# Sums of the seven-product weight factors: each written over another part, and issued one split ahead of its cast

## The chip, the cores and the metric

The kernel runs on one core of a Trainium2 chip. The metric is the device time of one execution in microseconds (us); of the kernel before there are three runs, with a median of 2215.59 us.

The engines are TensorE (PE: matrix products; PEld its weight loads), VectorE (DVE), ScalarE (ACT), GpSimd (POOL) and SyncE (SP, which issues most DMAs). Each engine works through its own queue in the order of the program. An instruction whose semaphores are not up yet holds up all that stands behind it in the same queue.

## What is computed

One inference step of a two-layer trunk: an mLSTM mixer with a SwiGLU feed-forward part, then sliding-window attention with a second SwiGLU part, for 1024 prompt rows and 32 sample rows of width 1024. Nothing but the two feed-forward parts is touched by the change:

```python
def swiglu(x, w_gu, w_down):
    g, u = jnp.split(x @ w_gu, 2, axis=-1)
    return (jax.nn.silu(g) * u) @ w_down
...
x = layer_norm(DEEPNORM_ALPHA * x + swiglu(x, w_gu[layer], w_down[layer]), ln_g[layer, 1], ln_b[layer, 1])
```

`w_gu` is 1024 x 5632 in each layer, `w_down` 2816 x 1024, all in float32.

## The kernel before

**Three products for one.** Each float32 operand is split in a high part, rounded to the matrix unit's type by a cast, and a low part, the difference. `gemm` (lines 360 to 371) issues high x high, high x low and low x high for every 128-row tile. A weight split is one cast on ACT (line 208) and one difference on POOL, for some weights on DVE (line 210).

**Seven products for eight.** Most of the feed-forward weights come in pairs of loaded units, `a` and `b`, each of 128 x 1024. Their halves a1, a2, b1, b2 (128 x 512) are the blocks of a 2 x 2 block matrix. Strassen's scheme in Winograd's form takes seven products of such blocks in place of eight. Its weight factors are four of the blocks' own and sums of them: a1, a2, b2, s1 = b1 + b2, s2 = s1 - a1, s3 = a1 - b1, s4 = a2 - s2. They are split in the order of `FACTORS` (line 135): a1, a2, b2, s2, s1, s3, s4. They are used in the order a1, a2, s2, b2, s1, s3, s4.

**Where the sums are made.** All four are 128 x 512 subtractions or additions on DVE, in place in the loaded tiles. `_source` issues them just ahead of the split that it is called for: `a1 -= b1` at b2's split (line 176, this is s3), `b1 += b2` and `b2 -= a1` at s2's split (lines 179 and 180, s1 and s2), `a2 -= b2` at s1's split (line 182, s4). The second of s2's sums overwrites b2, so it has to wait until b2's cast and difference, issued one split before, have read it.

**When a split is issued.** There are five buffers for split parts (`SLOTS`). In the stretches with pairs no split is paced by time: `done` (line 234), called when the products of a factor have been issued, takes the factor off the list and issues the next splits until four are held. So a split runs four factors ahead of PE: with the products of s3 of a pair behind it, `done` issues b2 of the next pair, with those of s4 its s2, with a1's the next s1, with a2's s3, and with s2's s4.

**The up stage** (`up_tile`, lines 342 to 401, 20 pairs in each layer) computes gate and up columns. A factor is 24 matmuls of 264 columns over 4 tiles and two column halves. The banks are of two kinds, A and B, two buffers each. In A a sum of products grows over a1, s2, s1 and s4, and ACT copies it out between them (lines 1362, 1372, 1379), which PE's next product in A has to wait for. B takes a2, b2 and s3, and DVE adds it to the copies (lines 1367, 1375, 1382, 1383; line 1384 multiplies gate and up, line 1390 is the second gate's activation and line 1397 its product). `done` for a factor stands ahead of these instructions. Beside this `stage` splits the results as the next product's moving operand and writes them to memory (cast at line 1288, difference at 1289, DMA at 1290; sums at 1300 to 1313).

**The down stage** (`down`, lines 1480 to 1521, 8 pairs in each layer). A factor is two halves (q) of 12 matmuls. Each half has a bank: A keeps one buffer per half over a1, s2, s1, s4, and B takes a2, b2, s3. After each half DVE puts the bank into the residual (`put`, lines 1487 to 1493), once or, for s3, twice. The next half into the same buffer waits for the put that reads it. A pair's first half writes the buffer that s4's first half of the pair before wrote. Here `done` follows the puts of the factor:

```python
                for q in range(2):
                    ...
                    for row, par in outs:
                        put(ps, 4 * j + 2 * q + row, par)
                ...
                W.done(u, f)
```

**Names in the trace.** `wr` are loaded units, `wh` and `wl` split parts (`_a`, `_b`, `_s` from the factor's first letter), `z` and `ex`, `sx` buffers of activations, `act` the residual, `hs_x` and `hs_t` the staged operands in memory.

Of the kernel before, what the change touches and what calls it, by code (L numbers as in the profile page):

```python
# [69 lines left out]
class Weave:  # L70


    def __init__(self):
        self.tasks = []
        self.feed = None
# [53 lines left out]
class Weights:  # L129
# [7 lines left out]
    def __init__(self, nc, pool, units, pairs, on_vector):  # L137
        self.nc, self.pool, self.units, self.on_vector = nc, pool, units, on_vector
        self.nload = self.njob = 0
        self.raw, self.parts, self.home, self.live = {}, {}, {}, set()  # L140
        self.jobs, self.last = [], {}
        self.wait, self.ahead, self.pause = 0.0, False, FEED_W
        self.depth = RAW - 1
        self.spare, self.spared = None, set()
        u = 0
        while u < len(units):
            if u in pairs:
                self.jobs += [(u, f) for f in self.FACTORS]
                self.last[u] = self.last[u + 1] = len(self.jobs) - 1
                u += 2  # L150
            else:
                self.jobs += [(u, 0), (u, 1)]
                self.last[u] = len(self.jobs) - 1
                u += 1
# [11 lines left out]
    def _source(self, u, f):  # L166

        n = self.units[u].shape[-1] // 2
        if f in (0, 1):
            return self.raw[u][:, f * n : (f + 1) * n]  # L170
        sub, add = self.nc.vector.tensor_sub, self.nc.vector.tensor_add
        a, b = self.raw[u], self.raw[u + 1]
        a1, a2, b1, b2 = a[:, :n], a[:, n : 2 * n], b[:, :n], b[:, n : 2 * n]
        if f == "b2":

            sub(a1, a1, b1)
        elif f == "s2":

            add(b1, b1, b2)
            sub(b2, b2, a1)  # L180
        elif f == "s1":
            sub(a2, a2, b2)
        return {"a1": a1, "a2": a2, "b2": b2, "s1": b1, "s2": b2, "s3": a1, "s4": a2}[f]

    def _next(self):
        if self.njob == len(self.jobs):
            return False
        key = self.jobs[self.njob]
        u, f = key
        if key not in self.home and len(self.live) == SLOTS and (self.spared or not self.spare):  # L190
            return False
        if key in self.home and any(self.home.get(k) is self.home[key] for k in self.parts):
            return False
        self.load_to(u if f in (0, 1) else u + 1)
        r = self._source(u, f)
        w = r.shape[-1]
        if key in self.home:
            hi, lo = self.home[key]
        else:
            if self.spare and not self.spared:  # L200
                self.spared.add(key)
                at, tag, bufs = self.spare, "x", 1
            else:
                self.live.add(key)
                at, tag, bufs = self.pool, "", SLOTS
            hi = at.tile([P, WD // 2], F32R, name=f"wh{u}_{f}", tag="wh" + tag, bufs=bufs)[:, :w]
            lo = at.tile([P, WD // 2], F32R, name=f"wl{u}_{f}", tag="wl" + tag, bufs=bufs)[:, :w]
        self.nc.scalar.copy(hi, r)  # L208
        eng = self.nc.vector if key in self.on_vector else self.nc.gpsimd
        eng.tensor_sub(lo, r, hi.bitcast(F32))  # L210
        self.parts[key] = (hi, lo)
        self.njob += 1
        if f in (1, "s4"):
            del self.raw[u]
            if f == "s4":
                del self.raw[u + 1]
                u += 1
            self.load_to(u + self.depth)
        return True

    def split_to(self, i):
# [1776 lines left out]
```

## Time and profile before

| | us |
|---|---|
| median of 3 runs (lowest, highest) | 2215.59 (2215.38, 2216.78) |
| the profiled execution, its own time | 2219.82 |
| its span, first to last instruction | 2218.0 |
| PE busy in the span | 2178.0 |
| DVE busy | 1468.7 |
| POOL busy | 1020.5 |
| ACT busy | 1002.6 |

The granted TensorE clock of the profiled execution is 0.997. A row of instructions names its line, engine and operation, then output<-input by the program's names, the shapes and a count, then the time in which the group was busy, the mean length of one in ns, and the idle time of the engine just before them with the instruction that ended most of it. In a timeline a row begins with start and length in us from the start of the span; instructions of the same kind in a row are merged, with their count. Matmuls overlap in their records, so the distance from start to start tells PE's pace, and not their length.

### The profile page before, as it was taken

Reading aid. Unit: us, or ns where it says so; the run is one execution under the profiler, and the core shown is the slowest. Engines: PE = TensorE matmul, PEld = TensorE weight load, DVE = VectorE, ACT = ScalarE, POOL = GpSimd, SP = SyncE. Lnnn points to the kernel's source line nnn. Section 1 sums busy time; section 2 is a strip of 40 time slices with the busy share of each in tenths; the row PEclk is TensorE's granted clock in tenths of the full one; section 3 lists DMA queues with packets and bytes.
Section 4 is the critical chain, followed back from the end, with each engine's and each line's share of the span. In section 5 each row is a group of like instructions: output and inputs, shape, how many; then the busy total and the mean of one; then the engine's idle time right before and its main releaser. Section 6 shows DMA issues by size and latency. Waiting matters only on the chain.

```text
span 2218.0 us, 44293 instructions
## 1 busy us (share of the span) xinstructions
PE 2178.0 (98%) x17086; PEld 2149.8 (97%) x17086; DVE 1468.7 (66%) x2848; ACT 1002.6 (45%) x2259; POOL 1020.5 (46%) x982
## 2 busy tenths in 40 slices
PE   9999999999999999999998999999999999999997
PEld 9999999999999999999998999899999999999997
DVE  4465677787666665566667678888576666466657
ACT  4443455464344444321245778756444444422125
POOL 2544210004666566544525776600576666554441
PEclk9999999999999999999999999999999999999999
DMA  5221212212443343797515333521244434397712
GB/s 169 78 62 57 57 39 86 89 39 80 153 155 136 137 155 136 248 333 230 175 57 173 108 100 97 155 63 39 103 162 163 135 138 155 129 343 258 243 59 79
DMA packets 174500, 298.10 MB, mean 134 GB/s; under 512 B 18065, under 2 KB 130761, under 8 KB 174289
## 3 DMA queue, kind: packets, MB, share of 16 engines
q1 hardware_dynamic: 169936, 290.94, 39.9%
q10 hardware_dynamic: 4352, 4.33, 0.6%
q8 instruction: 135, 2.21, 0.4%
q14 instruction: 77, 0.62, 0.1%
HBM read 201.80 MB, written 82.94 MB: 128 GB/s over the span
## 4 chain that ended last, share of the span: by engine, by line
PE 61%; DVE 5%; ACT 3%; DMA 2%; issue 2%; POOL 2%; SPq 0%; POOLq 0%; DVEq 0%; ACTq 0%
PE A L368 9%; PE A L370 9%; PE A L369 9%; PE B L368 6%; PE B L369 6%; PE B L370 6%; PE d L368 4%; PE d L370 4%; PE d L369 4%; PE T L1763 1%; POOL s L1743 1%; DMA hs_x<-z 1%; DMA sx<-hs_t 1%; ACT act L471 1%; PE O L1778 1%
## 5 line engine op out<-in xcount | busy, mean ns | idle before, releaser
L210 POOL TENSOR_TENSOR wl_s<-wr,wh_s 128x512 fp32r<-128x512 f32 x224 | 316.6, 1433 | 262.6 <-ACT wh_s L208 187.6
L210 POOL TENSOR_TENSOR wl_a<-wr,wh_a 128x512 fp32r<-128x512 f32 x112 | 168.7, 1513 | 386.7 <-ACT wh_a L208 264.5
L368 PE MATMUL d<-sx,wh 128*128 128x264 f32 (+2 forms) x1068 | 341.3, 320 | 2.1 <-ACT wh L208 1.6
L370 PE MATMUL d<-sx,wl 128*128 128x264 f32 (+2 forms) x1068 | 325.7, 305 | 2.8 <-POOL wl L210 2.8
L369 PE MATMUL d<-sx,wh 128*128 128x264 f32 (+2 forms) x1068 | 324.8, 304 | 0.4 <-DVE sx L399 0.4
L208 ACT CAST wh_s<-wr 128x512 fp32r<-128x512 f32 x224 | 136.0, 619 | 323.4 <-DVE wr L180 295.6
L368 PE MATMUL A<-sx,wh_s 128*128 128x264 f32 x896 | 254.8, 284 | 1.8 <-ACT z L1372 1.8
L369 PE MATMUL A<-sx,wh_s 128*128 128x264 f32 x896 | 254.2, 284 | 0.0
L370 PE MATMUL A<-sx,wl_s 128*128 128x264 f32 x896 | 254.0, 284 | 0.0
L368 PEld LDWEIGHTS d<-sx,wh 128*128 128x128 f32 x1068 | 201.9, 189 | 5.8 <-ACT wh L208 2.3
L370 PEld LDWEIGHTS d<-sx,wl 128*128 128x128 f32 x1068 | 201.3, 189 | 4.2 <-POOL wl L210 3.9
L369 PEld LDWEIGHTS d<-sx,wh 128*128 128x128 f32 x1068 | 202.1, 189 | 1.5 <-DVE sx L399 0.7
L368 PE MATMUL d<-sx,ex 128*128 128x264 f32 x624 | 180.5, 289 | 0.1
L369 PE MATMUL d<-sx,ex 128*128 128x264 f32 x624 | 177.2, 284 | 0.0
L370 PE MATMUL d<-sx,ex 128*128 128x264 f32 x624 | 176.9, 284 | 0.0
L368 PEld LDWEIGHTS A<-sx,wh_s 128*128 128x128 f32 x896 | 168.4, 188 | 2.4 <-ACT z L1372 2.2
L370 PEld LDWEIGHTS A<-sx,wl_s 128*128 128x128 f32 x896 | 168.8, 188 | 0.0
L369 PEld LDWEIGHTS A<-sx,wh_s 128*128 128x128 f32 x896 | 168.4, 188 | 0.0
L1289 POOL TENSOR_TENSOR z<-z 128x528 fp32r<-128x528 f32 x76 | 104.8, 1378 | 113.4 <-ACT z L1288 106.8
L210 POOL TENSOR_TENSOR wl<-wr,wh 128x512 fp32r<-128x512 f32 (+2 forms) x81 | 104.1, 1293 | 93.1 <-ACT wh L208 89.3
L1743 POOL TENSOR_SCALAR s<-s,st 128x256 f32<-128x256 f32 (+1 forms) x144 | 123.1, 867 | 47.9 <-DVE st L1741 32.0
L1288 ACT CAST z<-z 128x528 fp32r<-128x528 f32 x136 | 86.1, 633 | 94.2 <-DVE z L1301 39.1
(348 smaller groups left out, 7307.3 us busy)
## 6 DMA issues: line engine op xcount, KB each, us to landing
wr<-in_gu SPq DMA_DIRECT2D x92, 512.0 KB
hs_x<-z SPq DMA_DIRECT2D x72, 528.0 KB
hs_t<-z SPq DMA_DIRECT2D x64, 528.0 KB
sx<-hs_x SPq DMA_DIRECT2D x112, 264.0 KB
sx<-hs_t SPq DMA_DIRECT2D x64, 264.0 KB
ex<-hs_t SPq DMA_DIRECT2D x64, 264.0 KB
wr<-in_dn SPq DMA_DIRECT2D x32, 512.0 KB
ex<-hs_x SPq DMA_DIRECT2D x32, 264.0 KB
```

Of the source, the lines that this page charges most:

```text
L208: self.nc.scalar.copy(hi, r)
L210: eng.tensor_sub(lo, r, hi.bitcast(F32))
L368: nc.tensor.matmul(out, ah, bh, start=start and k == 0, stop=False, **kw)
L369: nc.tensor.matmul(out, ah, bl, start=False, stop=False, **kw)
L370: nc.tensor.matmul(out, al, bh, start=False, stop=stop and k == last, **kw)
L471: nc.scalar.activation(z, z, AF.Identity, scale=gk, bias=bk)
L1288: nc.scalar.copy(hi.bitcast(F32R), buf(s))
L1289: eng.tensor_sub(lo.bitcast(F32R), buf(s), hi)
L1743: nc.gpsimd.tensor_scalar_mul(p[:R, h, lo:256], p[:R, h, lo:256], st[:R, 2, h : h + 1])
L1763: nc.tensor.transpose(pt[:nk, i, h, :R], p[:R, h, c : c + nk], ident[:R, :R])
L1778: nc.tensor.matmul(po[:, :, :R], v, s["hi"][:nk, i, :, :R], start=(i == 0), stop=False)
```

## The change

The same four sums are made from other parts. s1 still goes over b1. s2 is now b1 - a1 and goes over a1, s3 is b2 - s2 and goes over b2, and s4 is a2 - s2 over a2. No sum overwrites a part whose split has been issued immediately before it. They are issued by a new function, `prepare`, which `_next` calls at its end for the split that comes next, and which `_source` calls where this has not happened. So the two sums for s2 stand behind the split of b2, the one for s3 behind the split of s1, and the one for s4 behind the split of s3. The order of the splits is as before.

```diff
+        self.made = set()
...
         if f in (0, 1):
             return self.raw[u][:, f * n : (f + 1) * n]
+        self.prepare(u, f)
+        a, b = self.raw[u], self.raw[u + 1]
+        return {
+            "a1": a[:, :n], "a2": a[:, n : 2 * n], "b2": b[:, n : 2 * n],
+            "s1": b[:, :n], "s2": a[:, :n], "s3": b[:, n : 2 * n], "s4": a[:, n : 2 * n],
+        }[f]
+
+    def prepare(self, u, f):
+
+        if (u, f) in self.made or f not in ("s2", "s3", "s4"):
+            return
+        self.made.add((u, f))
         sub, add = self.nc.vector.tensor_sub, self.nc.vector.tensor_add
+        n = self.units[u].shape[-1] // 2
         a, b = self.raw[u], self.raw[u + 1]
         a1, a2, b1, b2 = a[:, :n], a[:, n : 2 * n], b[:, :n], b[:, n : 2 * n]
-        if f == "b2":
-
-            sub(a1, a1, b1)
-        elif f == "s2":
-
+        if f == "s2":
             add(b1, b1, b2)
+            sub(a1, b1, a1)
+        elif f == "s3":
             sub(b2, b2, a1)
-        elif f == "s1":
-            sub(a2, a2, b2)
-        return {"a1": a1, "a2": a2, "b2": b2, "s1": b1, "s2": b2, "s3": a1, "s4": a2}[f]
+        else:
+            sub(a2, a2, a1)
...
             self.load_to(u + self.depth)
+        if self.njob < len(self.jobs):
+            u, f = self.jobs[self.njob]
+            if u in self.raw and u + 1 in self.raw:
+                self.prepare(u, f)
         return True
```

## The prediction

> **What bounds the kernel now.** I read the page first, then TensorE's (PE's) waits, the 14 places at which one down pair follows another, and the up stages' few gaps.
>
> ```profile
> span 2218.0 us, 44293 instructions
> PE 2178.0 (98%) x17086; PEld 2149.8 (97%) x17086; DVE 1468.7 (66%) x2848; ACT 1002.6 (45%) x2259; POOL 1020.5 (46%) x982
> L208 ACT CAST wh_s<-wr 128x512 fp32r<-128x512 f32 x224 | 136.0, 619 | 323.4 <-DVE wr L180 295.6
> ```
>
> PE is busy for 98% of the span, so 295.6 us of ScalarE (ACT) idling behind the sum of line 180 is mostly not a cost: what counts is where PE itself stops. The stretch and its busy times, then the waits of PE in the down stage of the first layer and the sums there (count; shortest, median, longest ns):
>
> ```profile
> 955.00:1090.00 135.00, 135.00 (x1114) 135.00 (x1113) 89.59 (x130) 28.38 (x48) 63.74 (x48) 1.00 0.75 243
> PE A L368 <- DVE act L1491: 1.1, 1, 1.1
> L176 DVE TENSOR_TENSOR wr<-wr,wr x6: 684/684/686, 971.9 to 1073.9; 128x512 f32<-128x512 f32 x6
> L176 DVE TENSOR_TENSOR wr<-wr,wr x6: 685/686/686, 2004.6 to 2106.5; 128x512 f32<-128x512 f32 x6
> ```
>
> PE has no visible hole in 135 us; VectorE (DVE) is busy for 89.59. But a busy average hides who arrives with nothing to spare. One boundary between two down pairs, on DVE, GpSimd (POOL) and PE (start, duration):
>
> ```profile
> 989.65 2.77 DVE L1493 TENSOR_TENSOR act<-act,B 128x528 f32<-128x528 f32 x4 [0.75 <-PE B L370]
> 992.34 0.68 DVE L176 TENSOR_TENSOR wr<-wr,wr 128x512 f32<-128x512 f32 x1
> 992.94 0.70 DVE L1493 TENSOR_TENSOR act<-act,A 128x528 f32<-128x528 f32 x1
> 994.00 0.71 DVE L1493 TENSOR_TENSOR act<-act,A 128x528 f32<-128x528 f32 x1 [0.36 <-PE A L370]
> 994.62 0.68 DVE L179 TENSOR_TENSOR wr<-wr 128x512 f32<-128x512 f32 x1
> 995.41 0.69 DVE L180 TENSOR_TENSOR wr<-wr,wr 128x512 f32<-128x512 f32 x1
> 996.02 0.70 DVE L1493 TENSOR_TENSOR act<-act,A 128x528 f32<-128x528 f32 x1
> ...
> 988.82 1.29 POOL L210 TENSOR_TENSOR wl_b<-wr,wh_b 128x512 fp32r<-128x512 f32 x1 [1.67 <-ACT wh_b L208]
> ...
> 993.68 0.28 PE L370 MATMUL A<-sx,wl_s 128*128 128x264 f32 x1
> 993.80 0.34 PE L368 MATMUL A<-ex,wh_a 128*128 128x264 f32 x1
> 993.98 0.28 PE L369 MATMUL A<-ex,wh_a 128*128 128x264 f32 x1
> ```
>
> The matmul at 993.80 opens the next pair and overwrites bank A's first buffer, which the put at 992.94 has to read out first (s4's first half). That put ends at 993.64, 0.16 before the matmul. At the first boundary, where PE does wait:
>
> ```profile
> 951.56 0.69 DVE L176 TENSOR_TENSOR wr<-wr,wr 128x512 f32<-128x512 f32 x1
> 952.16 1.31 DVE L1491 SCALAR_TENSOR_TENSOR act<-act,A 128x528 f32<-128x528 f32 x2
> ...
> 951.67 0.28 PE L370 MATMUL A<-sx,wl_s 128*128 128x264 f32 x1
> 953.01 0.36 PE L368 MATMUL A<-sx,wh_a 128*128 128x264 f32 x1 [1.06 <-DVE act L1491]
> 953.21 0.28 PE L369 MATMUL A<-sx,wh_a 128*128 128x264 f32 x1
> ```
>
> The first of the two puts lasts 952.16 + 0.70 (the other put's length) = 952.86, and PE goes 0.15 later. So a lag of 0.15 is the signal itself, and 0.16 at the steady boundary means that DVE meets PE's pace with 0.01 us left. I read PE as bounded by DVE's queue there, though no view calls it a wait.
>
> **The change part by part.** Four sums per pair before, four after; casts, differences on POOL and loads stay, and their order too. What moves is where the sums stand in DVE's queue.
>
> *Behind s3.* The split of the next pair's b2 is issued when s3's products are done. Before, one sum went with it (line 176, at 992.34). Now two do, `b1 += b2` and `a1 = b1 - a1`, the second needing the first. From L176 to the put is 0.60 start to start. From L179 to L180, where the second also waits for the first, is 995.41 - 994.62 = 0.79, and from L180 to the put 0.61. So the put of s4 moves from +0.60 to 0.79 + 0.61 = +1.40: 0.80 later. Queued behind it are s4's second put and a1's puts; who waits is PE's first matmul of the next pair. There are 8 down pairs in a layer, 7 boundaries, so 14 (the six L176 per window above and one at 951.56, twice). 14 x 0.80 = 11.2, less the slack: 0.01 at 993.80, none at the two waiting boundaries; I allow 0.02 at each of the other 12, 0.3 in all. **Loss 10.9.** Lower end: sums that start 0.60 apart, 14 x 0.60 - 0.3 = 8.1. Upper end: after a real wait PE's second matmul also comes late, 953.21 - 953.01 = 0.20 against a pitch of 0.12 (993.80 less 993.68), adding 0.08 at 12 boundaries: 11.9.
>
> The Trainium skill, VectorE: DVE Perf Modes, section The DRAIN you can't avoid, says that a semaphore between consecutive VectorE operations adds nothing to their distance. By it the second sum would start 0.60 after the first and the loss would be the 8.1. The rows disagree, 0.79 where one waits for the other, so I keep 0.80.
>
> *Behind s4.* L179 and L180 vanish there, 1.4 us of DVE. In the down stage the next puts wait for PE anyway (0.36 idle before 994.00), so it is worth nothing. If POOL's queue or ACT's were what PE awaited it would be worth up to 1.4 a pair; the down stage shows no such wait.
>
> *s3's and s4's sums.* `b2 -= a1` stands where line 182 stood (behind a1's products), `a2 -= a1` one factor on, behind a2's. In the down stage 0.7 to 1.8 us (the longest sum, below) goes ahead of s2's puts. Those have until s1 reuses their buffer, three half factors of 12 x 0.12 = 1.46, or 4.4 us, and take 0.70 each: covered; uncovered, it would cost up to 1.8 - 0.7 a pair. In the up stage it goes ahead of the addition at line 1367, whose bank is not wanted for several factors.
>
> *The cast freed.* s2's cast waits no longer on sums issued beside it. Here PE's gaps in the up stages matter: first tile, then third, of layer one.
>
> ```profile
> 526.93 0.28 PE L370 MATMUL B<-sx,wl_a 128*128 128x264 f32 x1
> 527.10 0.39 PE L368 MATMUL A<-ex,wh_s 128*128 128x264 f32 x1
> 527.32 0.28 PE L369 MATMUL A<-ex,wh_s 128*128 128x264 f32 x1
> 527.84 0.40 PE L370 MATMUL A<-ex,wl_s 128*128 128x264 f32 x1 [0.24 <-POOL wl_s L210]
> ...
> 574.22 0.28 PE L370 MATMUL B<-ex,wl_b 128*128 128x264 f32 x1
> 575.84 0.39 PE L368 MATMUL A<-sx,wh_s 128*128 128x264 f32 x1 [1.34 <-ACT z L1372]
> ```
>
> The first three intervals are 0.91 instead of 0.36: 0.55 lost, with 0.1 more on the restart. The other is 1.62 instead of 0.12: 1.50. Layer two, PE's waits in its up stage:
>
> ```profile
> PE A L368 <- ACT z L1372: 0.4, 1, 0.4
> PE A L368 <- ACT z L1362: 0.2, 1, 0.2
> PE A L370 <- POOL wl_s L210: 0.2, 1, 0.2
> ```
>
> The wait view counts from a matmul's modelled end, 0.16 less than start to start (1.34 against 1.50), so these are about 0.6, 0.4 and 0.4. All four gaps hold 0.65 + 1.5 + 1.4 = 3.6. Why the third tile stalls:
>
> ```profile
> 564.58 0.69 DVE L180 TENSOR_TENSOR wr<-wr,wr 128x512 f32<-128x512 f32 x1
> ...
> 565.36 0.62 ACT L208 CAST wh_s<-wr 128x512 fp32r<-128x512 f32 x1 [6.64 <-DVE wr L180]
> 565.88 0.60 ACT L1390 ACTIVATE z<-A 128x528 f32<-128x528 f32 x1
> ...
> 567.84 1.79 DVE L1289 TENSOR_TENSOR z<-z 128x528 fp32r<-128x528 f32 x1
> ...
> 574.14 0.63 ACT L1288 CAST z<-z 128x528 fp32r<-128x528 f32 x1 [0.76 <-DMA hs_t<-z]
> ...
> 575.20 0.59 ACT L1372 COPY z<-A 128x528 f32<-128x528 f32 x1
> ```
>
> ACT sits 6.64 on the cast with the activation of line 1390 right behind, then a staging write, its DMA, and the copy for which PE waits. With both sums ahead of lines 1382 to 1384 the activation comes earlier, and the copy has 1.5 us to win. **Gain**: the first tiles in full (0.65 and 0.8), two thirds of the third tiles' 2.1, since line 1289 and the DMA may start less early: 2.9. Ends: 0, and 3.6. Late next would be the same copy; the three rows are all of PE's waits in that stage, so nothing else there is near its path.
>
> *Contended sums.* In the up stage a sum beside POOL takes longer:
>
> ```profile
> 638.84 1.77 DVE L176 TENSOR_TENSOR wr<-wr,wr 128x512 f32<-128x512 f32 x1
> 643.14 0.70 DVE L1382 TENSOR_TENSOR z<-z,B 128x528 f32<-128x528 f32 x1 [2.53 <-PE B L370]
> ```
>
> Two of these are 3.5 us, until 642.4, inside the 2.53 us for which DVE waits for s3's products before line 1382: nothing. Without that cover they would delay line 1382 by up to 1.8 a tile, whose bank PE wants only several factors later.
>
> **The sum.** 10.9 - 2.9 = +8.0 on the profiled execution's 2219.82 (span 2218.0 and 1.8 around it): 2227.8. That execution lies 4.2 above the median of the three runs, 2215.59, so the forecast for the median is **2223.6**. Ends: 8.1 - 3.6 = +4.5, 2220.1; and +11.9, 2227.5.
>
> **The rivals.** *Misplaced sums (the other side).* The two sums could come out a factor away from s3's puts, if the count of held parts put b2's split elsewhere. Then the put follows s3's puts at once, no boundary pays, the two waiting ones even win 0.60: -1.2 - 2.9 = -4.1, 2211.5. It decides from the point where DVE's queue has no sum between line 1493's four puts and s4's. For it: nothing but that the function is called anew. Against: L176 stands there in all rows, and the number of splits held is untouched.
>
> *Nothing extra for the dependence.* 8.1 - 2.9 = +5.2, 2220.8. Against it the 0.79. That is the rule of the Trainium skill named above.
>
> *Contention at the boundary.* If a POOL difference ran under the two sums, each could take 1.77 and not 0.68: one or both of them 1.09 longer at 14 places, 15 to 31 us on top of the 8, 2239 to 2254. Against: b2's difference ends at 990.11, 2.2 us before the sums. The Trainium skill, SBUF — State Buffer, section Who interferes with whom, has a VectorE operation with two SBUF inputs fully blocked by a GpSimd one that reads SBUF. The 1.77 agrees; only a moved POOL operation would bring it here.
>
> *The gain falls out.* The freed cast could let staging reach its DMA no earlier: +10.9, 2226.5.
>
> **How the numbers follow.** The forecast's case 0.72 (own range 2221 to 2226.5), the gain falling out 0.08, no price for dependence 0.06, misplaced 0.09, contended 0.05. What a measurement here can tell from no change is 0.2%, 4.4 us: 2211.2 to 2220.0. Slower: 0.72 + 0.08 + 0.05, and two thirds of 0.06, less 0.04 for the forecast case's tail, 0.85. Misplaced divides evenly at its -4.1: 0.05 faster, and the remaining 0.10 is same. For 8 in 10 the range runs from 2219.0 to 2228.0: it leaves out misplaced, contended and thin tails.
>
> **What would show it.** Between line 1493's four puts and s4's first put, two sums with a put 1.4 after the first; a wait of PE of about 0.8 at each of 14 boundaries, named after DVE's lines 1491 and 1493; no wait of ACT on the line of the sums like the 295.6; PE's waits at s2 in the first tiles gone, and at line 1372 smaller. Wrong: boundaries without a gap, a different sum there, or durations of 1.8.

## The result and the profile after

The changed kernel takes 2224.3 us (median of 6 runs, 2223.07 to 2229.09), the kernel before, on the same chip, 2217.16 (6 runs, 2215.38 to 2219.97). The ratio is 1.0035, with a 95% interval from 1.0022 to 1.0048: slower by 7.1 us. The prediction was 2223.6, with a range of 2219.0 to 2228.0.

The page of the changed kernel (its profiled execution took 2223.39 us): span, busy times, and the group of the weight casts, now line 219.

```profile
span 2221.5 us, 44254 instructions
PE 2177.9 (98%) x17086; PEld 2150.1 (97%) x17086; DVE 1448.6 (65%) x2848; ACT 1008.5 (45%) x2259; POOL 985.0 (44%) x982
L219 ACT CAST wh_s<-wr 128x512 fp32r<-128x512 f32 x224 | 136.8, 618 | 226.4 <-DVE wr L192 64.0
```

Most of the page looks better. DVE and POOL are busy for less, and the row of ACT's casts names 64.0 us of idling behind a sum where it named 295.6. (A row names its largest wait only. With 29.7 and 13.8 us behind the other sums ACT idles 107.5 us.) PE, the one that counts, has not changed its busy time and has a longer span.

Stage by stage it becomes plain. The timeline of PE, first in the kernel before, then in the changed one: the first matmul of the up stage, the first of the down stage and the last of the down stage, in layer one.

```profile
521.21 0.28 PE L368 MATMUL A<-sx,wh_a 128*128 128x264 f32 x1
...
931.49 0.28 PE L368 MATMUL A<-sx,wh_a 128*128 128x264 f32 x1
...
1095.73 0.28 PE L370 MATMUL A<-sx,wl_s 128*128 128x264 f32 x1
```

```profile
520.62 0.28 PE L383 MATMUL A<-sx,wh_a 128*128 128x264 f32 x1
...
928.66 0.28 PE L383 MATMUL A<-sx,wh_a 128*128 128x264 f32 x1
...
1098.62 0.28 PE L385 MATMUL A<-sx,wl_s 128*128 128x264 f32 x1
```

The up stage (`up_tile`, lines 1342 to 1401 of the kernel before) takes 928.66 - 520.62 = 408.04 instead of 410.28, the down stage 169.96 instead of 164.24. The same distances for both layers of every kernel of this study follow, in us, each from one profiled execution (five kernels repeat 408.04 and 408.30 to 0.01); "sum" is the difference of the four stages to the kernel before, "median" the difference of the medians, each to the kernel before on the same chip:

| kernel | up 1 | down 1 | up 2 | down 2 | sum | median |
|---|---|---|---|---|---|---|
| before | 410.28 | 164.24 | 410.00 | 164.65 | | |
| changed | 408.04 | 169.96 | 408.30 | 169.62 | +6.8 | +7.1 |
| e1_in_place | 412.58 | 164.27 | 412.43 | 163.53 | +3.6 | +2.3 |
| e2_two_sooner | 408.04 | 165.33 | 408.31 | 165.34 | -2.2 | -1.5 |
| e3_old_sums_ahead | 408.04 | 173.35 | 408.31 | 171.26 | +11.8 | +14.2 |
| e4_one_more | 410.86 | 170.96 | 410.96 | 169.31 | +12.9 | +11.9 |
| e5_up_ahead | 408.04 | 163.44 | 408.31 | 164.07 | -5.3 | -5.8 |
| e6_one_more_late | 409.75 | 164.13 | 409.65 | 164.20 | -1.4 | +0.3 |
| e7_one_each | 408.04 | 167.39 | 408.30 | 167.33 | +1.9 | +1.0 |

The change loses 5.72 + 4.97 = 10.69 in the down stages and gains 2.24 + 1.70 = 3.94 in the up stages. (The two spans differ by 3.5 only, because the first stage began 0.59 earlier and the stretch between the layers, which the change doesn't touch, took 455.29 instead of 457.95. That stretch lies between 455.1 and 459.4 in the nine profiles.)

The boundary that the prediction showed, in the changed kernel, on DVE, ACT, POOL and PE:

```profile
988.65 2.77 DVE L1508 TENSOR_TENSOR act<-act,B 128x528 f32<-128x528 f32 x4 [0.75 <-PE B L385]
991.34 0.69 DVE L189 TENSOR_TENSOR wr<-wr 128x512 f32<-128x512 f32 x1
992.11 0.69 DVE L190 TENSOR_TENSOR wr<-wr,wr 128x512 f32<-128x512 f32 x1
992.72 1.31 DVE L1508 TENSOR_TENSOR act<-act,A 128x528 f32<-128x528 f32 x2
...
992.90 1.14 ACT L219 CAST wh_s<-wr 128x512 fp32r<-128x512 f32 x2 [5.16 <-PE A L384]
...
987.81 1.29 POOL L221 TENSOR_TENSOR wl_b<-wr,wh_b 128x512 fp32r<-128x512 f32 x1 [1.66 <-ACT wh_b L219]
...
992.68 0.28 PE L385 MATMUL A<-sx,wl_s 128*128 128x264 f32 x1
993.57 0.36 PE L383 MATMUL A<-ex,wh_a 128*128 128x264 f32 x1 [0.61 <-ACT wh_s L219]
993.76 0.29 PE L384 MATMUL A<-ex,wh_a 128*128 128x264 f32 x1
```

Two sums stand between s3's four puts and s4's first. The second starts 0.77 after the first, and the put at 992.72, 1.38 after the first sum. With the 0.70 of one put it ends at 993.42, and PE goes 0.15 later, at 993.57. PE's distance is 0.89 where it was 0.12, and the next matmul comes 0.19 later and not 0.12. All twelve boundaries without a wait before now have 0.82 to 0.89; the two that had one went from 1.34 to 2.27 and from 1.46 to 1.97.

PE's waits, over the whole span (total us, times, longest), name another engine:

```profile
PE A L383 <- ACT wh_s L219: 10.5, 14, 2.0
```

Fourteen waits, as many as boundaries, and 10.5 us, but put down to ACT's cast of s2. The matmul at 993.57 reads `wh_a`, not `wh_s`, which speaks against it; but the first of the two casts at 992.90, 0.62 long, ends at 993.52 and the put at 993.42, so time alone doesn't tell the two apart here. The other places say more. In all six waits of PE for ACT that the profile of the kernel before shows, PE starts 0.05 after the end of the cast or copy. Here it starts 0.05 after the end of the cast at eight of the fourteen places, but 0.01 after it at the other six (the second, fourth and sixth boundary of each layer), which is too soon. Behind the end of the put the lag is 0.15 at the eight and 0.10 at the six. That speaks for the put; whether the put or the cast holds PE is the first question to the experiments.

### The profile page after: what moved, and what is told of

Same layout as the page of the kernel before. It is cut to its first block, busy times and chain, and to the rows that moved or that the text cites. A ratio compares the mean times of both kernels' runs of the same rounds, so it can differ in the third digit from the quotient of the medians.

```text
span 2221.5 us, 44254 instructions
## 1 busy us (share of the span) xinstructions
PE 2177.9 (98%) x17086; PEld 2150.1 (97%) x17086; DVE 1448.6 (65%) x2848; ACT 1008.5 (45%) x2259; POOL 985.0 (44%) x982
## 5 line engine op out<-in xcount | busy, mean ns | idle before, releaser
L221 POOL TENSOR_TENSOR wl_s<-wr,wh_s 128x512 fp32r<-128x512 f32 x224 | 298.7, 1337 | 267.3 <-ACT wh_s L219 256.9
L221 POOL TENSOR_TENSOR wl_a<-wr,wh_a 128x512 fp32r<-128x512 f32 x112 | 153.5, 1373 | 398.0 <-ACT wh_a L219 274.2
L383 PE MATMUL A<-ex,wh_s 128*128 128x264 f32 x448 | 127.4, 284 | 0.0
```

What stands on the lines that cost most here:

```text
L383: nc.tensor.matmul(out, ah, bh, start=start and k == 0, stop=False, **kw)
```

## The experiments

The theory: the price is DVE's queue at one place, the put of s4 behind s3's puts; whatever stands ahead of it there costs its length. Rivals: PE waits for s2's cast on ACT, as the wait view has it; or the kernel is slower for DVE's load or the new aliasing (s2 now goes over a1 and s3 over b2; s1 and s4 stay over b1 and a2), wherever the sums stand. The gain of the up stages is a second question: does it come from issuing ahead, or from the other parts? Diffs are against the changed kernel, except for e4 and e6, which are against the kernel before.

**e1_in_place: the new parts, each sum issued by its own split.**

```diff
-        if self.njob < len(self.jobs):
-            u, f = self.jobs[self.njob]
-            if u in self.raw and u + 1 in self.raw:
-                self.prepare(u, f)
```

> The new sums, but each issued at its own split, none ahead: s2's two sums then stand behind s4's puts, and no sum at all between s3's four puts and s4's first put. Theory (PE loses its time at the boundary between down pairs, to the sums in front of s4's first put): the twelve small boundaries close to 0.12 us, the two that already waited shrink from 1.34 and 1.46 by about 0.6 each, s2's cast waits for its sum again and the four gaps in the up stages (3.9 us) stay. Time: 1 us below the kernel before, +-2. Rival (the new sums themselves, with their longer chain of dependences, cost the time wherever they stand): 7 us above the kernel before, like the changed kernel.

Measured: 2220.26 (11 runs), ratio 1.001 (1.0001 to 1.0019). In the down stages the twelve boundaries are back at 0.12, as expected, and the two waiting ones shrink to 0.88 and 0.69. In layer one a distance of 0.72 ahead of the first pair's s4 takes the gain back (the kernel before has one of 0.30 at that place in layer two), so the stages are at 164.27 and 163.53. The sign of the whole was missed, because the up stages became 2.3 and 2.4 *longer* than before. An up tile of this kernel, on DVE, ACT and PE:

```profile
634.71 0.71 DVE L1324 TENSOR_TENSOR z<-z 128x528 f32<-128x528 f32 x1 [2.65 <-POOL z L1300]
635.34 0.69 DVE L194 TENSOR_TENSOR wr<-wr 128x512 f32<-128x512 f32 x1
...
636.11 0.62 ACT L219 CAST wh_s<-wr 128x512 fp32r<-128x512 f32 x1 [2.85 <-DVE wr L194]
636.64 0.59 ACT L1383 COPY z<-A 128x528 f32<-128x528 f32 x1
...
637.29 0.39 PE L379 MATMUL A<-sx,wh_s 128*128 128x264 f32 x1 [0.19 <-ACT z L1383]
```

s4's sum (line 194) stands in DVE's queue behind a staging sum that waits 2.65 for POOL. So s4's cast waits 2.85, and the copy for which PE waits stands right behind the cast on ACT. This recurs in every second tile from the fourth to the sixteenth. With other parts alone, then, the down stage pays nothing and the up stage gains nothing: place decides both.

**e2_two_sooner: s2's sums behind a1's split, two splits before their own.**

```diff
-        if self.njob < len(self.jobs):
+        if key[1] == "a1":
+            self.load_to(key[0] + 1)
+            self.prepare(key[0], "s2")
+        elif self.njob < len(self.jobs):
             u, f = self.jobs[self.njob]
-            if u in self.raw and u + 1 in self.raw:
+            if f != "s2" and u in self.raw and u + 1 in self.raw:
```

> The new sums; the two for s2 are issued two splits sooner still, behind the split of a1 instead of the split of b2, the others as in the changed kernel. On DVE they then stand behind b2's puts and ahead of s1's. Theory: no sum in front of s4's first put, so the twelve boundaries close to 0.12, the other two shrink by 1.4 from 2.27 and 1.97, the gaps in the up stages stay closed, and s1's puts, up to 2 us late beside POOL, still have time. Time: 5 us below the kernel before (-3.9 for the up stages, -1.2 for the two boundaries), +-2. Rival (PE waits for ACT's cast of s2 at the boundary, as the wait view names it, or for DVE's load as a whole): the boundaries stay at 0.8, 7 us above the kernel before.

Measured: 2216.41 (11 runs), ratio 0.9994 (0.9985 to 1.0003): a gain of 5 us was expected, and none is clear of the noise. The up stages keep all of theirs, the twelve boundaries are at 0.12, but each layer's first down pair has a new gap of 1.80 and 1.67 ahead of s4. DVE there:

```profile
941.69 1.09 DVE L189 TENSOR_TENSOR wr<-wr 128x512 f32<-128x512 f32 x1
945.21 0.69 DVE L190 TENSOR_TENSOR wr<-wr,wr 128x512 f32<-128x512 f32 x1 [2.44 <-POOL wl_a L221]
945.82 1.79 DVE L1307 TENSOR_TENSOR z<-z 128x528 fp32r<-128x528 f32 x1
947.54 1.30 DVE L1509 SCALAR_TENSOR_TENSOR act<-act,A 128x528 f32<-128x528 f32 x2
```

s2 goes over a1, so its sum must wait until POOL has read a1 for the difference: 2.44 us at the head of DVE's queue, with the staging of line 1307 and then a put behind it. Right behind its split an operand is not yet free.

**e3_old_sums_ahead: the sums and parts of the kernel before, issued one split ahead.**

```diff
-            "s1": b[:, :n], "s2": a[:, :n], "s3": b[:, n : 2 * n], "s4": a[:, n : 2 * n],
+            "s1": b[:, :n], "s2": b[:, n : 2 * n], "s3": a[:, :n], "s4": a[:, n : 2 * n],
...
-        if (u, f) in self.made or f not in ("s2", "s3", "s4"):
+        if (u, f) in self.made or f not in ("b2", "s2", "s1"):
...
+        if f == "b2":
+            sub(a1, a1, b1)
+        elif f == "s2":
             add(b1, b1, b2)
-            sub(a1, b1, a1)
-        elif f == "s3":
             sub(b2, b2, a1)
         else:
-            sub(a2, a2, a1)
+            sub(a2, a2, b2)
```

> The old sums, over the old parts, each issued one split ahead as in the changed kernel: s3's sum behind a2's split, s1's and s2's behind b2's, s4's behind s2's. The second sum behind b2's split again has to wait for b2's difference on POOL. Theory (place in DVE's queue alone decides): two sums with 0.8 between them in front of s4's first put, boundaries of 0.8, 5 to 9 us above the kernel before; in the up stages DVE may wait up to 2 us for POOL a tile, hidden. Rival (writing over other parts is what moved the time): within 2 us of the kernel before.

Measured: 2232.09 (5 runs), ratio 1.0065 (1.0053 to 1.0078), more than expected. The up stages are at 408.04 and 408.31, the changed kernel's to 0.01: the gain comes from issuing ahead, and the other parts add nothing to it. The twelve boundaries have 0.83 to 0.90, like the changed kernel. The excess lies at the two waiting boundaries, now 4.01 and 3.54. DVE at the first of them:

```profile
946.53 1.82 DVE L189 TENSOR_TENSOR wr<-wr,wr 128x512 f32<-128x512 f32 x1
948.28 2.53 DVE L1508 TENSOR_TENSOR act<-act,B 128x528 f32<-128x528 f32 x4
950.74 0.68 DVE L191 TENSOR_TENSOR wr<-wr 128x512 f32<-128x512 f32 x1
951.52 0.69 DVE L192 TENSOR_TENSOR wr<-wr,wr 128x512 f32<-128x512 f32 x1
952.13 1.31 DVE L1506 SCALAR_TENSOR_TENSOR act<-act,A 128x528 f32<-128x528 f32 x2
```

The subtraction of s3 (line 189) falls a factor earlier into a backlog of DVE, and takes 1.82 and not 0.69, beside a difference on POOL that starts 0.03 before it and lasts 1.31. So three sums, not two, are ahead of s4's put, and after the longer stall the clock was halved (below).

**e4_one_more: the kernel before, with one more DVE instruction at b2's split.** The instruction is the larger of a1 and a1, written over a1, which leaves the values as they are. ACT's casts, the aliasing and the other sums stay.

```diff
         if f == "b2":
             sub(a1, a1, b1)
+            self.nc.vector.tensor_tensor(a1, a1, a1, op=ALU.max)
```

> The kernel before with one more VectorE instruction of the same size behind line 176 in every pair, the maximum of a1 with itself, which leaves the values as they are and has to wait for the sum. Theory: the price of the boundary alone, without the freed cast: 14 boundaries 0.8 longer, 11 us above the kernel before, and the gaps in the up stages as before or larger. Rival (DVE has a third of its time free, 56 instructions more are hidden): within 2 us of the kernel before.

Measured: 2229.84 (5 runs), ratio 1.0057 (1.0044 to 1.0069): 11.9 us above the kernel before, where 11 were expected. The stages have 12.9: 11.4 in the down stages, of which some 1.5 are a stretch at half clock (below), and 1.5 in the up stages, which were left open. The same boundary on DVE, PE and ACT:

```profile
995.15 0.68 DVE L176 TENSOR_TENSOR wr<-wr,wr 128x512 f32<-128x512 f32 x1
995.87 0.69 DVE L177 TENSOR_TENSOR wr<-wr 128x512 f32<-128x512 f32 x1
996.48 1.31 DVE L1494 TENSOR_TENSOR act<-act,A 128x528 f32<-128x528 f32 x2
...
996.50 0.28 PE L371 MATMUL A<-sx,wl_s 128*128 128x264 f32 x1
997.33 0.36 PE L369 MATMUL A<-ex,wh_a 128*128 128x264 f32 x1 [0.55 <-DVE act L1494]
...
999.28 1.14 ACT L209 CAST wh_s<-wr 128x512 fp32r<-128x512 f32 x2 [7.73 <-DVE wr L181]
```

One instruction of 0.69 in an engine that idles a third of the span, and PE's distance at this place is 0.83 instead of 0.12. Here the wait view names DVE's put. The cast of s2 isn't the cause: in this kernel it starts at 999.28, 1.95 after the matmul, and PE stalls as in the changed one. At all fourteen places PE starts 0.15 or 0.10 after the put's end, at each with the lag that it has in the changed kernel, while the last cast of a weight ended over 5 us before.

**e6_one_more_late: the same instruction, at s2's split.**

```diff
             add(b1, b1, b2)
             sub(b2, b2, a1)
+            self.nc.vector.tensor_tensor(a1, a1, a1, op=ALU.max)
```

> The kernel before with the same one more VectorE instruction as in e4_one_more, in every pair, but behind s2's sums of line 180, which stand behind s4's puts and not in front of them. Theory (place, not load): down stages within 1 us of the kernel before, whole time 0 to 2 us above it, the 2 from a longer way of DVE in the up stages. Rival (load): 11 us above, as in e4_one_more.

Measured: 2218.11 (11 runs), ratio 1.0002 (0.9993 to 1.001). DVE around the boundary:

```profile
990.87 0.68 DVE L176 TENSOR_TENSOR wr<-wr,wr 128x512 f32<-128x512 f32 x1
991.47 0.69 DVE L1494 TENSOR_TENSOR act<-act,A 128x528 f32<-128x528 f32 x1
...
994.66 0.69 DVE L181 TENSOR_TENSOR wr<-wr 128x512 f32<-128x512 f32 x1
```

The same instruction as in e4 (line 181 here) costs nothing that can be measured one factor later, where the next puts wait for PE anyway: the down stages are 0.1 and 0.5 shorter than before. Ahead of s4's put it made them 6.7 and 4.7 longer. So it is the place, not DVE's load.

**e5_up_ahead: sums ahead in the up stages, by their own split in the down stages.** If both halves of the theory hold, this keeps the gain without the loss.

```diff
-            if u in self.raw and u + 1 in self.raw:
+            if u not in self.still and u in self.raw and u + 1 in self.raw:
...
+    W.still = {u for layer in U_DN for block in layer[:TAIL] for u in block}
```

> The changed kernel, but in the down pairs each sum is issued at its own split; in the up pairs one split ahead, as changed. Theory: the two effects are apart, so the up stages take the 408.0 and 408.3 us that they take in the changed kernel and the down stages the 164.3 and 163.5 that they take with every sum at its own split: 5 us below the kernel before, +-1.5, and faster than both kernels. Rival (the down stage needs the sums ahead, or the boundary's loss comes with the freed cast): 3 us or more above the kernel before.

Measured: 2211.99 (9 runs, the kernel before 2217.8), ratio 0.9972 (0.9963 to 0.9982): 5.8 us faster than the kernel before, and so faster than both. The boundary on DVE and PE:

```profile
987.95 2.77 DVE L1509 TENSOR_TENSOR act<-act,B 128x528 f32<-128x528 f32 x4 [0.75 <-PE B L386]
990.85 0.70 DVE L1509 TENSOR_TENSOR act<-act,A 128x528 f32<-128x528 f32 x1
...
992.92 0.68 DVE L189 TENSOR_TENSOR wr<-wr 128x512 f32<-128x512 f32 x1
...
991.98 0.28 PE L386 MATMUL A<-sx,wl_s 128*128 128x264 f32 x1
992.10 0.28 PE L384 MATMUL A<-ex,wh_a 128*128 128x264 f32 x1
```

s4's put stands right behind s3's, with no sum between. It ends at 990.85 + 0.70 = 991.55; with the lag of 0.15, PE could go at 991.70, and goes at 992.10 at its own pace. The slack is 0.40 where the kernel before had 0.01, and the two waiting boundaries shrink too, to 0.74 and 0.87. A distance of 0.42 stands ahead of the first pair's s4 in layer two, where the kernel before has 0.30.

**e7_one_each: one of s2's sums stays behind b2's split, the addition goes one split before it.**

```diff
         if f == "s2":
-            add(b1, b1, b2)
             sub(a1, b1, a1)
...
         if self.njob < len(self.jobs):
             u, f = self.jobs[self.njob]
             if u in self.raw and u + 1 in self.raw:
+                n = self.units[u].shape[-1] // 2
+                if f == "b2":
+                    b = self.raw[u + 1]
+                    self.nc.vector.tensor_add(b[:, :n], b[:, :n], b[:, n : 2 * n])
                 self.prepare(u, f)
```

> The changed kernel, with the addition b1 += b2 issued one split sooner still, behind a2's split, so that a single sum stands between s3's puts and s4's, as in the kernel before. Theory (0.8 for a second sum, nothing for the first): the twelve boundaries back at 0.12, the two large ones about 0.6 over the kernel before, up stages as in the changed kernel: 3 us below the kernel before, +-1.5. Rival (any sum of the new kind at the boundary delays PE because it waits for another): boundaries of 0.2 us or more, 0 to 3 us above the kernel before.

Measured: 2218.79 (11 runs), ratio 1.0003 (0.9994 to 1.0011): a gain of 3 us was expected, and none came. With one sum left at the place, the twelve boundaries close to 0.12, as the theory has it. But the two waiting ones grow to 2.91 and 2.85. DVE and PE at the first:

```profile
946.39 1.80 DVE L235 TENSOR_TENSOR wr<-wr 128x512 f32<-128x512 f32 x1
948.11 2.53 DVE L1511 TENSOR_TENSOR act<-act,B 128x528 f32<-128x528 f32 x4
...
949.10 0.28 PE L388 MATMUL A<-sx,wl_s 128*128 128x264 f32 x1
952.01 0.42 PE L386 MATMUL A<-sx,wh_a 128*128 128x264 f32 x1 [2.63 <-ACT wh_s L218]
952.23 0.42 PE L387 MATMUL A<-sx,wh_a 128*128 128x264 f32 x1
```

As in e3, the earlier sum falls into DVE's backlog from the up stage, where it takes 1.80 beside a POOL difference that starts 0.03 before it and lasts 1.28. And after the stall the matmuls go 0.22 apart and not 0.12: the clock, below.

## Why the prediction was right, and where it wasn't

**The loss (10.9 predicted, 10.69 measured): right, and for its reason.** The two sums are where they were said to be, 0.77 apart (0.79 predicted), and the put starts 1.38 behind the first (1.40). e4 shows the mechanism alone, e6 that place and not load makes it, e1 and e5 that it goes away with the sums. So the slack of 0.01, read from a boundary that no view called a wait, was real there. At the twelve boundaries the distance to the first matmul grew by 0.70 to 0.77 and the one to the second by 0.08 to 0.02, together 0.78 or 0.79 each, where 0.78 was put down. (The second matmul's lateness, kept for the upper end, was paid in part, because in the kernel before it stood at 0.12 to 0.18 already. The slack was not 0.02 everywhere: at the six boundaries with a lag of 0.10 it was 0.06 to 0.08.) The two waiting boundaries grew by 0.93 and 0.51, not 0.80 each. That the two layers together come within 0.2 us is in part luck.

**The price of the dependence: the row was right, not the rule.** At this boundary the second sum starts 0.77 behind the first, against 0.60 from an independent sum to the put. By the Trainium skill, VectorE: DVE Perf Modes, section The DRAIN you can't avoid, the semaphore would have added nothing; the trace disagrees by 0.17. (In e4, where the added instruction waits for the sum in front, it starts 0.72 behind it, so the price there is 0.12.)

**The gain (2.9 predicted, 3.94 measured): the mechanism right, one term too small.** The first tiles' gaps vanished, as said: no two successive matmuls of the changed kernel's up stages start more than 0.15 apart. The step that was mis-sized is "two thirds of the third tiles' 2.1": all of it went. The third tile of layer one in the changed kernel, on ACT and PE:

```profile
561.60 0.62 ACT L219 CAST wh_s<-wr 128x512 fp32r<-128x512 f32 x1 [4.14 <-PE A L385]
562.13 0.60 ACT L1405 ACTIVATE z<-A 128x528 f32<-128x528 f32 x1
...
570.25 0.62 ACT L1303 CAST z<-z 128x528 fp32r<-128x528 f32 x1
571.30 0.59 ACT L1387 COPY z<-A 128x528 f32<-128x528 f32 x1
...
573.09 0.28 PE L383 MATMUL A<-sx,wh_s 128*128 128x264 f32 x1
```

The activation now starts 3.75 earlier (562.13 for 565.88), the staging cast 3.89, the copy 3.90; 0.59 of each is the earlier start of the whole stage. So nothing of the lead was lost on the way through the staging and its DMA, which the prediction feared, and the copy ends at 571.89, 1.2 before the matmul that needs it. All of PE's gaps in those stages are gone. The prediction counted them as 3.6. Counted from start to start, with the late second matmul behind each, they are 2.2 in layer one and 1.7 in layer two, which is the whole 3.94. That e3 has the same up stages and e1 longer ones shows that issuing ahead is what does it.

**The rivals.** *Misplaced*: no; L189 and L190 stand in front of the put. *Contention at the boundary*: no; b2's difference ends at 987.81 + 1.29 = 989.10, 2.2 before the sums, and these take 0.69. But its price is real: 1.82 in e3 and 1.80 in e7, where a sum was moved beside a POOL difference. That is the rule of the Trainium skill, SBUF — State Buffer, section Who interferes with whom; the trace agrees, at another place than the rival's. *The gain falls out*: no.

**What was to show it.** The sums, their distance and the 14 waits came as described. The name did not: "a wait of PE of about 0.8 at each of 14 boundaries, named after DVE's lines 1491 and 1493" is put down to ACT's cast in the changed kernel. e4 has the same wait under DVE's name, with the cast out of the way, so the name in the changed kernel comes of two ends within some 0.1 us. ACT's idle time behind the sums fell from 295.6 to 107.5 us, and that was worth 3.94 us of PE's time and no more.

**The net.** +8.0 was predicted, +6.8 measured in the stages and +7.1 between the medians. That the forecast lies within 0.7 of 2224.3 is partly two errors that cancel: a base of three runs, 1.6 below the median that six gave, and a net 0.9 too large.

## What to carry to other kernels

A busy share doesn't show where an engine has no slack: take the end of the instruction that frees a buffer, add the lag that a real wait of the same kind shows, and compare it with the start of the matmul that reuses it; where the two meet, every instruction put ahead costs the time by which it delays that end (here 0.78 us for one sum that takes 0.69), however idle the engine is on average. Moving work ahead pays where a cast blocks a queue that PE waits for, and not where it lands ahead of a tight release, so it is to be decided stage by stage (e5 against the changed kernel: 2211.99 to 2224.3). The engine that a wait view names is the one whose signal came last in the record; where two end together, compare the lag with that of a real wait for the same engine, and a kernel that moves only one of the two tells which one holds.

## What the runs showed of the hardware

**The half clock went with the idle time inside one window, not with the length of the gap.** After some stalls PE's granted clock was 0.50 for 3.41 us. Stretches behind the first waiting boundary: e4 and e7, then the changed kernel (window, its length, busy us of PE, PEld, DVE, ACT and POOL with their instructions, the granted clock, DMA share, GB/s).

```profile
953.70:956.90 3.20, 3.20 (x15) 3.20 (x16) 1.99 (x4) 1.14 (x2) 0.71 (x1) 0.50 1.07 386
```

```profile
952.30:955.50 3.20, 3.20 (x16) 3.20 (x16) 0.79 (x2) 0.18 (x1) 2.25 (x2) 0.50 1.07 372
```

```profile
954.00:957.30 3.30, 3.30 (x29) 3.30 (x29) 2.03 (x4) 0.62 (x1) 0.81 (x1) 1.00 1.10 361
```

There are 15 or 16 matmuls in 3.20 us instead of some 26: about 15 of them come at 0.22 and not 0.12, so 1.5 us are lost. At the waiting boundaries it came after gaps (here from start to start of two matmuls) of 2.14 (e4), 2.91 and 2.85 (e7) and 4.01 (e3), and not after 3.54 (e3, layer two), 2.27 and 1.97 (changed) and 2.03 (e4, layer two). The changes of the granted clock within a profile all lie multiples of 3.413 us apart. For the next count 0.12, PE's own pace, is taken off the start of each gap. Laid on that grid, the longest share of each of these gaps that falls into one window was 2.02, 2.79, 2.66 and 2.40 where half clock followed in the next window, and 1.93, 1.37, 1.85 and 1.91 where none did. In all nine profiles, behind the start-up and up to 2205 us, every window with 2.02 us or more of PE's gaps (those that are over 0.25 us by this count) was followed by half clock, 19 of 19. Between the layers, where PE's work is thin, some with less were too (1.52 to 1.62 where the clock had been full until then), so this count alone does not sort those. The bound was read from these runs after the fact, it depends on this way of counting, and none was made to test it. The Trainium skill, TensorE: Matmul & The Clock Gate, section 🔬 Part 1: The HAM clock gate (the "warmup" mystery), calls the window free-running and 3413 ns long: the grid agrees. Its section 🎯 Why this matters for your kernels asks for no idle gap over about 3 us; here 2.14 was too long already, and 3.54 was not. The stretch between the layers has two to four such windows of half clock in each profile; whether that is why it varies from 455.1 to 459.4 was not tried.

**A sum beside POOL.** In the kernel before, the 134 sums of 128x512 that no TENSOR_TENSOR instruction of POOL overlaps take 0.68 or 0.69 each, and the 90 that one overlaps take 0.71 to 1.79. In e3 and e7 the two rows shown take 1.82 and 1.80.
